# Sharing the first squares of a hybrid attention layer between two engines, moving one weight cast and four differences

## The chip, the cores and the metric

The kernel runs on one core of a Trainium2 chip. The metric is the device time of one execution in microseconds (us). The engines are TensorE (PE; its weight loads are listed apart as PEld), VectorE (DVE), ScalarE (ACT), GpSimd (POOL) and SyncE (SP), which here only issues DMAs. Each engine works through a queue of its own in a fixed order.

## The reference, cut to what matters

One layer, 1,024 positions, width 1,024, all fp32:

```python
h = rms_norm(x, pre_g)                     # x * rsqrt(mean(x*x) + 1e-6) * pre_g
z = jnp.einsum('bsd,de->bse', h, w_in)     # w_in: 1024 x 7184
qa, ka, va, ga, qb, kb, vb, gb, gk_low = split_columns(z)
oa = diff_attention(...)                   # 8 heads, softmax differences
gk = gk_low @ w_gk_up + b_gk               # gk_low has 16 columns
ob = gla_chunked(qb, kb, vb, log_sigmoid(gk) / 16)
y = concat([oa, ob]) @ w_out
return x + rms_norm(y, post_g)
```

The change lies in the first 80 us: the norm of `x`, its transposition, and the beginning of the product with `w_in`.

## The kernel before, in words

**The input.** `x` is loaded in eight tiles of 128 rows by 1,024 columns (`load_x`, L596). For each of the first four, `norm_x` (L613) lets ScalarE square the tile and sum it along the row, then `rstd` (L1633) makes the reciprocal root: two small ScalarE steps (Ln, Exp; L1636, L1637) and three small VectorE steps (L1638, L1640, L1646). `scale_x` (L607) multiplies the tile by it: columns 0 to 511 on VectorE, columns 512 to 1,023 on GpSimd. The other four tiles are normed in pairs, and scaled by GpSimd alone.

**Transposition.** `first(h)` (L654) transposes half h of the columns of tiles 0 to 3 on TensorE into four PSUM banks, and `put` (L644) splits each bank into a high part (`h_hi`, ScalarE, rounded to fp32r, times `pre_g`) and a low part (`h_lo`, VectorE, the rest). `blocks(j)` (L679) does the same for tiles 4 to 7 and also makes sums and differences of the four blocks of `h` (`s1`, `s2`, `s3`, and at L771 `s4`). Products are done by seven block products in place of eight (`LEFT`, L383, says which block each takes), so sums and differences of `w_in` are needed too.

**Weights.** `prepare(i)` (L283) makes the weights of step i of `order` (L243): a ScalarE cast to a high part (L379) and a VectorE subtraction to a low part (L380), after a VectorE subtraction where a difference of blocks is wanted. Steps 0 and 1 share a pair of tiles, as do 2 and 3, so `prepare(0..3)` casts twice. `go(n)` (L739) takes n steps; each prepares up to three steps ahead, then `multiply` (L395) issues 24 or 12 matmuls. TensorE's order is the program's (L142). While `pinned[0]` is set (L638 to `first(1)`, and for the beginning of the first `blocks`), the orders of ScalarE, VectorE and GpSimd are the program's too. Later they are chosen by the compiler's schedule, which goes by its own estimate of times, within the data's dependencies; `issue_after` puts a floor under single instructions.

**Idle products.** `spin` (L388) issues matmuls on a zero tile between the transposes of the first tiles, so that TensorE isn't idle until the first product.

**The low-rank gate.** `low_rank_weights` (L786) loads `w_gk_up` and 16 columns of `w_in` by GpSimd's queue into tiles `gk_up` and `wd`, and splits them on VectorE into `up` (a part of tile `ku`) and `wl`; `low_rank` (L808) multiplies with them.

The order around the change:

```python
for i in range(4):
    prepare(i)
first(0)
norm_x(4, 5)
norm_x(6, 7)
...
go(1)
first(1)
```

Of the kernel before, what the change touches and what calls it, by code (L numbers as in the profile page):

```python
# [8 lines left out]
F32 = mybir.dt.float32  # L9
F32R = mybir.dt.float32r  # L10
AF = mybir.ActivationFunctionType
ALU = mybir.AluOpType
PSUM = bass.MemoryType.PSUM

P = 128
S = 1024
D = 1024
# [5 lines left out]
EPS = 1e-6  # L23
# [8 lines left out]
def hymba_kernel(  # L32
# [20 lines left out]
    nc = tc.nc  # L53
# [21 lines left out]
    act, dve, pool = Queue(nc.scalar), Queue(nc.vector), Queue(nc.gpsimd)  # L75
# [4 lines left out]
    def cols(half):  # L80
        return slice(half * 512, half * 512 + 512)
# [3 lines left out]
    hw = ctx.enter_context(tc.tile_pool(name="hw", bufs=1, side="right", reuse_waits="tile"))  # L85
    const = ctx.enter_context(tc.tile_pool(name="const", bufs=1))
# [8 lines left out]
    eps_t = const.tile([P, 1], F32, name="eps_t")  # L95
# [33 lines left out]
    def bank(i, shape, name):  # L129
        return psum.tile(shape, F32, tag=f"b{i}", name=name)  # L130
# [4 lines left out]
    def take_bank(shape, name):  # L135
        i = free.pop(0)
        return bank(i, shape, name), i
# [3 lines left out]
    def mm(*a, **k):  # L141
        tc.keep_in_program_order(pe.matmul(*a, **k))  # L142

    def tr(dst, src):
        tc.keep_in_program_order(pe.transpose(dst, src, ident))  # L145
# [114 lines left out]
    i = order.index((1, 4))  # L260
# [22 lines left out]
    def prepare(i):  # L283

        if i >= len(order) or i in ws:
            return
        if 4 <= i <= n_early + 1:
            with tc.issue_after(act.last), tc.issue_after(dve.last):
                make_weights(i)
        elif order[i] in ((0, 6), (0, 4)):  # L290
            with tc.issue_after(behind[2 if order[i] == (0, 6) else 0].ins):
                make_weights(i)
        else:
            make_weights(i)
# [44 lines left out]
    def make_weights(i):  # L339
        p, n = order[i]  # L340
        if (wide(p) and p % 2) or p == VALS[1]:
            ws[i] = ws_wide[p - 1, n]
            return
        if p in VALS:
            ws[i] = ws_wide[p, n] = value_weights(n)
            return
        if p in early and n < 3:
            src = early[p][n - 1]
        else:
            fetch_raw(p, n, i)  # L350
            if wide(p):
                (b11, b21), (b12, b22) = ([raws[q].get(kh) for kh in range(2)] for q in (p, p + 1))
            else:
                top, bot = raws[p][0], raws[p][1]
                b11, b12 = top[:, :, :P], top[:, :, P:]
                b21, b22 = bot[:, :, :P], bot[:, :, P:]


            def sub(dst, a, b):
                dve.tensor_tensor(dst, a, b, ALU.subtract)  # L360
                return dst

            if n == 5:
                src = sub(b11, b12, b11)
            elif n == 6:
                src = sub(b11, b22, b11)
            elif n == 4:
                src = sub(b21, b21, b11)
            elif n == 7:
                src = sub(b12, b22, b12)  # L370
            else:
                src = {1: b11, 2: b21, 3: b22}[n]
        if wide(p):
            w = [ap.tile([P, HB, 256], F32R, tag="ring", name="w", bufs=NRING) for _ in range(2)]
            ws_wide[p, n] = w
        else:
            w2 = ap.tile([P, 2, HB, P], F32R, tag="ring", name="w", bufs=NRING)
            w = [w2[:, 0], w2[:, 1]]
        act.copy(w[0], src)  # L379
        dve.tensor_tensor(w[1], src, fp(w[0]), ALU.subtract)  # L380
        ws[i] = w
# [6 lines left out]
    def spin(n):  # L388

        if not spins:  # L390
            spins.append(bank(free[-1], [P, 512], "spin"))
        for i in range(n):
            mm(spins[0], ones, idle, start=(i == 0), stop=(i == n - 1))
# [200 lines left out]
    xs, x2 = [], []  # L594
# [12 lines left out]
    def scale_x(st, cs, engine=pool):  # L607
        x_cs = xs[st][:, cs]
        return engine.tensor_scalar(x_cs, x_cs, norms[st], 1.0, ALU.mult, ALU.mult)

    norms = {}

    def norm_x(*sts):  # L613
        n = len(sts)
        ssq = const.tile([P, 4, n], F32, tag=f"ssq{sts[0]}", name="ssq", bufs=1)
        for i, st in enumerate(sts):
            junk = hw.tile([P, D], F32, tag=("s2_hi0", "s2_lo0")[st % 2], name="junk")
            act.activation(
                junk, xs[st], AF.Square, scale=D**-0.5, accum_out=ssq[:, 0, i : i + 1]
            )  # L620
        rstd(nc, ssq[:, :, :n], ssq[:, 0, :n], eps_t, tc.keep_in_program_order)
        for i, st in enumerate(sts):
            norms[st] = ssq[:, 1, i : i + 1]
            if n == 1:
                scale_x(st, cols(0), dve)
            else:
                scale_x(st, slice(0, D))
# [8 lines left out]
    load_early(2)  # L636
    load_early(4)
    pinned[0] = True  # L638
    for st in range(4):
        norm_x(st)  # L640
    for st in range(4):
        scale_x(st, cols(1))

    def put(ps, k, dst, j):  # L644
        hi, lo = dst
# [6 lines left out]
    f1 = [hpool.tile([P, HB, 512], F32, tag=f"s4_{n}0", name=f"f1{n}") for n in ("hi", "lo")]  # L652

    def first(h):  # L654

        ps = [take_bank([P, 512], "xT") for _ in range(HB)]
        if not h:
            spin(14)
        for i in range(4):
            for j in range(HB):  # L660
                k = h * HB + j
                tr(ps[j][0][:, i * P : (i + 1) * P], xs[i][:, k * P : (k + 1) * P])
            if not h:
                spin((3, 7, 3, 4)[i])
        hi, lo = H[("h11", "h12")[h]]
        for j in range(HB):
            put(ps[j][0], h * HB + j, (hi, lo), j)
        pinned[0] = not h
        for j in range(HB):
            if h:  # L670
                act.activation(f1[h][:, j], ps[j][0], AF.Copy, scale=pre_g[:, h * HB + j : h * HB + j + 1])
            free.append(ps[j][1])
# [78 lines left out]
                if fill and next(fill[0], 0) == 0:  # L751
                    fill.pop(0)

    for i in range(4):
        prepare(i)
    first(0)
    norm_x(4, 5)
    norm_x(6, 7)
    for j in range(HB):
# [11 lines left out]
    s4 = [kp.tile([P, 2, 512], F32, tag=f"k{i}", name="s4") for i in range(2)]  # L771
    with tc.issue_after(behind[0].ins), tc.issue_after(behind[1].ins):
        for j in range(HB):
            dve.tensor_tensor(s4[j // 2][:, j % 2], f1[1][:, j], f1[0][:, j], ALU.subtract)
    for j in range(HB):
        parts("s4", j, s4[j // 2][:, j % 2])

# [3 lines left out]
    up, keep = ku[:, 0], fp(ku)[:, 1]  # L781

    wl2 = kp.tile([P, KT + HB, 64], F32R, tag="q0", name="wl2")
    R = GK_RANK

    def low_rank_weights():  # L786

        pool.memset(keep, 1.0)
        pool.memset(keep.rearrange("p (c i) -> p c i", i=64)[:, :, 0:1], 0.0)
        gk_up = t_c("gk_up")[:R]  # L790
        pool.dma_start(gk_up, w_gk_up[0])
        wd = t_c("wd").rearrange("p (k r) -> p k r", r=R)
        wd, wl = wd[:, KT : KT + HB], wd[:, :KT]
        pool.dma_start(wl, w_in[0, :, GKL : GKL + GK_RANK].rearrange("(k p) c -> p k c", p=P))
        pool.memset(fp(wl2), 0.0)
        pool.memset(fp(gkl), 0.0)
        pool.memset(fp(up), 0.0)
        with tc.issue_after(behind[0].ins):
            dve.tensor_tensor(wd, wl[:, HB:], wl[:, :HB], ALU.subtract)
            for dst, src in ((wl2[:, :KT], wl), (wl2[:, KT:], wd)):  # L800
                dve.tensor_copy(dst[:, :, :R], src)
                dve.tensor_tensor(dst[:, :, 32 : 32 + R], src, fp(dst[:, :, :R]), ALU.subtract)
            dve.tensor_copy(up[0:R], gk_up)
            dve.tensor_copy(up[32 : 32 + R], gk_up)
            dve.tensor_tensor(up[64 : 64 + R], gk_up, fp(up[0:R]), ALU.subtract)
            dve.tensor_tensor(up[96 : 96 + R], gk_up, fp(up[0:R]), ALU.subtract)

# [825 lines left out]
def rstd(nc, t, s, eps, pin=None):  # L1633

    pin = pin or (lambda ins: ins)
    pin(nc.scalar.activation(t[:, 1], s, AF.Ln, bias=eps))  # L1636
    exp = pin(nc.scalar.activation(t[:, 1], t[:, 1], AF.Exp, scale=-0.5))  # L1637
    half = pin(nc.vector.tensor_scalar(t[:, 2], s, eps, -0.5, ALU.add, ALU.mult))  # L1638
    if t.shape[2] == 1:
        pin(nc.vector.scalar_tensor_tensor(  # L1640
            t[:, 2], t[:, 1], t[:, 2], t[:, 1], ALU.mult, ALU.mult
        ))
    else:
        pin(nc.vector.tensor_tensor(t[:, 2], t[:, 2], t[:, 1], ALU.mult))
        pin(nc.vector.tensor_tensor(t[:, 2], t[:, 2], t[:, 1], ALU.mult))
    last = nc.vector.scalar_tensor_tensor(  # L1646
        t[:, 1], t[:, 2], 1.5, t[:, 1], ALU.add, ALU.mult
    )
    return exp, pin(last), half
# [32 lines left out]
```

## Time and profile before

| | us |
|---|---|
| median of three runs | 973.23 (973.07 to 973.25) |
| span of the profiled execution, first to last instruction | 971.1 |
| TensorE busy / VectorE / ScalarE / GpSimd | 958.7 / 735.5 / 604.6 / 207.9 |
| first product on real data | begins at 13.70 |
| low-rank product | begins at 74.13 |

For the profiled execution itself no time beside its span is listed; the median of the runs lies 2.1 us above the span. Times in the profile count from the span's first instruction. A group's line has the busy time, the mean of one instruction in ns, and the idle time of the engine before them with what ended it. In a timeline, a row has start, length, engine, line, operation, output and inputs, and in brackets the idle time ahead of it. Nearly all ScalarE, VectorE and GpSimd work is recorded under L66, since it passes through one helper; tiles tell it apart. The shapes read "partitions x columns". A sum along the row shows as a second small instruction behind the main one (`ACTIVATION_READ_ACCUMULATOR` on ScalarE, `DVE_READ_ACCUMULATOR2_ANT` on VectorE); the kernel's existing `tensor_tensor_reduce` shows as `CUSTOM_DVE_ANT_0`.

### The profile page before, as it was taken

The page shows a single profiled execution, that of the slowest core. Times are in us where ns is not written, and L with a number is a line of the kernel's source. Part 1 is how long each engine was busy: PE and PEld are TensorE (multiplying, and loading weights), DVE is VectorE, ACT ScalarE, POOL GpSimd, SP SyncE. Part 2 cuts the span into 40 slices and gives each one's busy share as a digit, 9 for nine tenths or more (in the row PEclk, how much of TensorE's full clock was granted, in tenths as well). Part 3 has the DMA queues.
Part 4 walks back from the last instruction along what each step waited for, and adds up shares of the span by engine and source line. Part 5 has one row for each costly group of instructions (what it writes and reads, how often), then busy time and mean ns, then how long its engine had stood idle before and what let it go on. Part 6 is the DMA issues. An engine that isn't in the chain of part 4 may idle for free.

```text
span 971.1 us, 15096 instructions
## 1 busy us (share of the span) xinstructions
PE 958.7 (99%) x4977; PEld 814.5 (84%) x4977; DVE 735.5 (76%) x1464; ACT 604.6 (62%) x1166; POOL 207.9 (21%) x266
## 2 busy tenths in 40 slices
PE   8999999999999999999999999999999999999997
PEld 7998988888888888888888888878888888888786
DVE  5996698897687686686766576587888888898554
ACT  8752364764667555576665344366786787887773
POOL 4300001212141221231100002121322222443322
PEclk9999999999999999999999999999999999999999
DMA  9433366578568987986754588996656769994777
GB/s 347 163 103 117 101 192 225 170 239 294 199 210 255 300 272 251 302 277 212 259 177 152 163 251 269 401 336 203 221 170 218 241 200 355 334 286 106 152 210 148
DMA packets 151293, 220.39 MB, mean 227 GB/s; under 512 B 15728, under 2 KB 86384, under 8 KB 151120
## 3 DMA queue, kind: packets, MB, share of 16 engines
q1 hardware_dynamic: 137056, 178.70, 56.8%
q0 software_dynamic: 14160, 40.74, 14.5%
q8 instruction: 39, 0.64, 0.3%
q14 instruction: 38, 0.31, 0.1%
HBM read 133.93 MB, written 88.60 MB: 229 GB/s over the span
## 4 chain that ended last, share of the span: by engine, by line
PE 94%; ACT 3%; DVE 1%; issue 1%; DMA 0%; POOL 0%; DVEq 0%; ACTq 0%; POOLq 0%
PE x L142 23%; PE z L142 16%; PE y L142 16%; PE ypart L142 13%; PE sc L142 7%; PE po L142 5%; PE yps L142 4%; PE wtr L145 3%; PE gpo L142 3%; PE kv L142 1%; ACT junk L66 1%; PE gkl_ps L142 1%; PE pa L142 1%; DVE p L66 1%; ACT h_hi L66 0%
## 5 line engine op out<-in xcount | busy, mean ns | idle before, releaser
L66 ACT CAST w<-w_raw 128x512 fp32r<-128x512 f32 (+1 forms) x150 | 98.0, 655 | 92.3 <-PE y L142 46.4
L66 DVE TENSOR_TENSOR w<-w_raw,w 128x512 fp32r<-128x512 f32 (+1 forms) x150 | 109.3, 732 | 48.8 <-ACT w L66 44.6
L66 ACT ACTIVATE p<-p,stt 128x896 f32<-128x896 f32 (+7 forms) x128 | 99.3, 777 | 36.2 <-DVE stt L66 35.2
L66 ACT COPY s<-x 128x512 f32<-128x512 f32 x82 | 47.8, 586 | 88.8 <-PE x L142 88.2
L66 POOL TENSOR_SCALAR p<-p,stt,lam 128x1024 f32<-128x1024 f32 (+3 forms) x64 | 56.2, 879 | 147.7 <-DVE stt L66 143.8
L66 DVE CUSTOM_DVE_ANT_0 p<-sc,maskt 128x512 f32<-128x512 f32 (+3 forms) x128 | 74.3, 585 | 14.2 <-PE sc L142 12.9
L66 POOL DMA_DIRECT2D wo_d<-wo_hi x32 | 17.5, 545 | 313.9 <-ACT wo_hi L66 313.9
L142 PE MATMUL z<-s_hi,w 128*128 128x512 f32 x320 | 80.2, 393 | 0.0
L142 PE MATMUL x<-s_hi,w 128*128 128x512 f32 x320 | 80.1, 392 | 0.0
L142 PE MATMUL y<-h_hi,w 128*128 128x512 f32 x320 | 80.0, 392 | 0.0
L142 PE MATMUL ypart<-wo_hi,m_hi 128*128 128x512 f32 x192 | 79.5, 414 | 0.1
L142 PE MATMUL ypart<-wo_hi,m_lo 128*128 128x512 f32 x192 | 75.5, 393 | 0.0
L142 PE MATMUL ypart<-wo_lo,m_hi 128*128 128x512 f32 x192 | 75.4, 393 | 0.0
L142 PE MATMUL sc<-k,q 128*128 128x512 f32 (+1 forms) x192 | 69.1, 363 | 1.4 <-DVE stt L66 1.3
L142 PEld LDWEIGHTS z<-s_hi,w 128*128 128x128 f32 x320 | 59.7, 188 | 12.3
L142 PEld LDWEIGHTS y<-h_hi,w 128*128 128x128 f32 x320 | 59.7, 188 | 12.3
L142 PEld LDWEIGHTS x<-s_hi,w 128*128 128x128 f32 x320 | 59.7, 188 | 12.3
L66 DVE TENSOR_TENSOR w_raw<-w_raw 128x512 f32<-128x512 f32 (+1 forms) x88 | 66.1, 751 | 1.9 <-DMA w_raw<-in_w_in_dram 0.8
L142 PE MATMUL sc<-ks,q 128*128 128x512 f32 (+1 forms) x192 | 66.0, 347 | 0.0
L66 ACT CAST wt_hi<-wtr 128x512 fp32r<-128x512 f32 (+1 forms) x80 | 42.8, 535 | 25.1 <-PE wtr L145 24.3
L66 DVE TENSOR_TENSOR wt_lo<-wtr,wt_hi 128x512 fp32r<-128x512 f32 (+1 forms) x80 | 50.6, 633 | 8.9 <-ACT wt_hi L66 8.2
L66 DVE TENSOR_TENSOR c<-z,s 128x512 f32<-128x512 f32 x48 | 32.8, 688 | 30.6 <-ACT s L66 20.3
(225 smaller groups left out, 2351.7 us busy)
## 6 DMA issues: line engine op xcount, KB each, us to landing
w_raw<-in_w_in_dram SPq DMA_DIRECT2D x48, 512.0 KB, 4.9
wo_d<-wo_hi POOLq DMA_DIRECT2D x32, 256.0 KB, 3.8
q<-q_d SPq DMA_DIRECT2D x32, 256.0 KB, 4.7
k<-k_d SPq DMA_DIRECT2D x32, 256.0 KB, 5.5
ks<-k_d SPq DMA_DIRECT2D x64, 128.0 KB, 6.0
v<-v_d SPq DMA_DIRECT2D x16, 512.0 KB, 7.0
wo_raw<-in_w_out_dram POOLq DMA_DIRECT2D x31, 256.0 KB, 4.8
wo_d<-gqd POOLq DMA_DIRECT2D x22, 256.0 KB, 4.2
```

Of the source, the lines that this page charges most:

```text
L66: ins = op(*a, **k)
L142: tc.keep_in_program_order(pe.matmul(*a, **k))
L145: tc.keep_in_program_order(pe.transpose(dst, src, ident))
```

## The change

Five edits. (1) The loop over the first four tiles becomes `norm_first`: ScalarE squares the whole of tile 0 and the left halves of tiles 2 and 3; VectorE squares and sums, by `tensor_tensor_reduce`, the whole of tile 1 and the right halves of tiles 2 and 3. A right half's sum starts from 1e-6 and stands in for the epsilon of `rstd`. Tiles 0 and 1 have their left columns scaled by GpSimd, tiles 2 and 3 by VectorE. (2) The idle products are 18, 1, 1, 1, 3 instead of 14, 3, 7, 3, 4. (3) `prepare(2)` and `prepare(3)` stand behind `first(0)`. (4) The four differences `s4` are made by GpSimd. (5) Two copies of `gk_up` into `up` are made by ScalarE.

```diff
-    for st in range(4):
-        norm_x(st)
-    for st in range(4):
-        scale_x(st, cols(1))
+    def square(st, half, s, init):
+        cs = cols(half)
+        junk = hw.tile([P, 512], F32, tag=("s1_lo0", "s1_lo1")[half], name="junk_h")
+        if half:
+            dve.tensor_tensor_reduce(
+                junk, xs[st][:, cs], xs[st][:, cs], 1.0 / D, init, ALU.mult, ALU.add, s
+            )
+        else:
+            act.activation(junk, xs[st][:, cs], AF.Square, scale=D**-0.5, accum_out=s)
+
+    def norm_first():
+
+        ssq = [const.tile([P, 5, 1], F32, tag=f"ssq{st}", name="ssq", bufs=1) for st in range(4)]
+        whole = hw.tile([P, D], F32, tag="s2_hi0", name="junk")
+        act.activation(whole, xs[0], AF.Square, scale=D**-0.5, accum_out=ssq[0][:, 0])
+        whole = hw.tile([P, D], F32, tag="s2_lo0", name="junk")
+        dve.tensor_tensor_reduce(
+            whole, xs[1], xs[1], 1.0 / D, 0.0, ALU.mult, ALU.add, ssq[1][:, 0]
+        )
+        for st in range(4):
+            t = ssq[st]
+            eps = eps_t if st < 2 else t[:, 4]
+            if st == 1:
+                square(2, 1, ssq[2][:, 4], EPS)
+            elif st > 1:
+                square(st, 0, t[:, 0], None)
+            if st == 2:
+                square(3, 1, ssq[3][:, 4], EPS)
+            rstd(nc, t[:, :4], t[:, 0], eps, tc.keep_in_program_order)
+            norms[st] = t[:, 1]
+            scale_x(st, cols(0), dve if st > 1 else pool)
+        for st in range(4):
+            scale_x(st, cols(1))
+
+    norm_first()
...
-            spin(14)
+            spin(18)
...
-                spin((3, 7, 3, 4)[i])
+                spin((1, 1, 1, 3)[i])
...
-    for i in range(4):
+    for i in range(2):
         prepare(i)
     first(0)
+    for i in range(2, 4):
+        prepare(i)
...
-            dve.tensor_tensor(s4[j // 2][:, j % 2], f1[1][:, j], f1[0][:, j], ALU.subtract)
+            pool.tensor_tensor(s4[j // 2][:, j % 2], f1[1][:, j], f1[0][:, j], ALU.subtract)
...
-            dve.tensor_copy(up[0:R], gk_up)
-            dve.tensor_copy(up[32 : 32 + R], gk_up)
+            act.copy(up[0:R], gk_up)
+            act.copy(up[32 : 32 + R], gk_up)
```

## The prediction

> **What bounds the kernel now.** I read the page first, for the busy shares and the chain that ended last.
>
> ```profile
> span 971.1 us, 15096 instructions
> PE 958.7 (99%) x4977; PEld 814.5 (84%) x4977; DVE 735.5 (76%) x1464; ACT 604.6 (62%) x1166; POOL 207.9 (21%) x266
> PE 94%; ACT 3%; DVE 1%; issue 1%; DMA 0%; POOL 0%; DVEq 0%; ACTq 0%; POOLq 0%
> ```
>
> TensorE carries 94% of the chain and is busy 99% of the span, so only time in which TensorE stands still can be won, and 971.1 - 958.7 = 12.4 us of it exist. The change touches the first 75 us alone; the second view, busy time by stretches, shows where the standstills are (columns: stretch, length, then busy time and instructions of PE, PEld, DVE, ACT, POOL, granted clock, DMA share, GB/s).
>
> ```profile
> 13.60:24.00 10.40, 10.11 (x75) 8.99 (x75) 8.19 (x18) 10.27 (x22) 4.41 (x4) 1.00 1.11 405
> 24.00:58.00 34.00, 33.92 (x261) 32.35 (x260) 32.59 (x45) 23.38 (x39) 10.93 (x12) 1.00 0.43 136
> 58.00:63.60 5.60, 4.56 (x40) 4.36 (x38) 5.54 (x11) 4.44 (x7) 0.00 (x0) 1.00 0.52 140
> 63.60:971.10 907.50, 898.79 (x4562) 760.27 (x4562) 683.41 (x1377) 556.50 (x1081) 186.62 (x235) 1.00 0.72 228
> ```
>
> Up to 13.6 us there is no product yet. From 13.6 to 24 us ScalarE is full (10.27 of 10.40). From 24 to 58 us TensorE is full and VectorE nearly so. From 58 to 63.6 us TensorE loses 1.04 us while VectorE is full. So a change of this part acts through two places. The chain, in order of time, and the weight loads show both.
>
> ```profile
> 13.05 2.32 ACT h_hi L66 x4
> 15.38 2.08 ACT junk L66 x4
> ...
> 21.13 2.33 ACT h_hi L66 x4
> ```
>
> ```profile
> 23.51 0.65 PEld L142 LDWEIGHTS y<-w,h_hi 128*128 128x128 f32 x5 [0.28 <-ACT h_hi L66]
> ...
> 61.32 1.03 PEld L142 LDWEIGHTS y<-w,h_hi 128*128 128x128 f32 x8
> 63.60 0.53 PEld L142 LDWEIGHTS y<-w,h_hi 128*128 128x128 f32 x4 [1.24 <-DVE w L66]
> ```
>
> First place: until 23.5 us ScalarE's queue sets the pace, its last piece being the second group of block casts (`h_hi` from 21.13), which TensorE already awaits by 0.28 us. Second place: at 63.60 TensorE waits 1.24 us for a low weight part from VectorE.
>
> **Part 1, squares shared, second weight cast moved.** The rows of the last tile of the four, and what follows:
>
> ```profile
> 9.47 1.04 ACT L66 ACTIVATE junk<-x 128x1024 f32<-128x1024 f32 x1
> 10.64 0.21 DVE L1638 TENSOR_SCALAR ssq<-ssq,eps_t 128x1 f32<-128x1 f32 x1
> 11.08 1.98 ACT L66 CAST w<-w_raw 128x1024 fp32r<-128x1024 f32 x2
> 11.20 0.22 DVE L1640 SCALAR_TENSOR_TENSOR ssq<-ssq 128x1 f32<-128x1 f32 x1 [0.35 <-ACT ssq L1637]
> 11.46 0.16 DVE L1646 SCALAR_TENSOR_TENSOR ssq<-ssq 128x1 f32<-128x1 f32 x1
> 11.65 0.49 DVE L66 TENSOR_SCALAR x<-x,ssq 128x512 f32<-128x512 f32 x1
> 11.77 0.93 POOL L66 TENSOR_SCALAR x<-x,ssq 128x512 f32<-128x512 f32 x1 [0.68 <-ACT ssq L1637]
> 12.14 1.63 DVE L66 TENSOR_TENSOR w<-w_raw,w 128x1024 fp32r<-128x1024 f32 x1
> 12.19 0.42 PEld L145 LDWEIGHTS xT<-ident,x 128*128 128x128 f32 x4 [0.23 <-DVE x L66]
> 12.96 2.41 ACT L66 ACTIVATE h_hi<-xT,pre_g 128x512 fp32r<-128x512 f32 x4
> ```
>
> ScalarE now does four whole squares one after the other; each ends in two small activations and three small VectorE steps. In the new order VectorE takes the whole of tile 1 and a half each of tiles 2 and 3, all in one fixed queue with the small steps of every tile. The nearest rows for the new reduction are the kernel's own, on one operand in PSUM and one in SBUF, and a two-operand step of 1,024 columns:
>
> ```profile
> L66 DVE CUSTOM_DVE_ANT_0 p<-sc,maskt 128x512 f32<-128x512 f32 x80 | 54.9, 686 | 12.6 <-PE sc L142 11.9
> L66 DVE DVE_READ_ACCUMULATOR2_ANT stt<- 128x1 f32 x192 | 15.9, 83 | 0.0
> L66 DVE TENSOR_TENSOR t<-b,t 128x1024 f32<-128x1024 f32 x4 | 4.9, 1220 | 0.2 <-ACT t L66 0.2
> ```
>
> A half is 0.69 + 0.08 = 0.77 us, a whole 1.22 + 0.08 = 1.30 us. It can't begin before tile 1 is there (row of its load alone: issued at 1.3, 4.6 us to landing, so 5.9):
>
> ```profile
> L604 SPq DMA_DIRECT2D x<-in_x_dram x1: 415/415/415, 1.3 to 1.3; - x1
> ...
> DMA to landing us min/median/max: 4.6/4.6/4.6
> ```
>
> The small steps of one tile take 0.24 (the 0.21 step and a gap), 11.46 - 11.20 = 0.26 and 11.65 - 11.46 = 0.19: 0.69 us. VectorE then runs: tile 1 whole to 7.2; steps of tile 0 to 7.9; half of tile 2 to 8.65; steps of tile 1 to 9.35; half of tile 3 to 10.1; steps of tile 2 to 10.8; its scaling (0.49) to 11.3; steps of tile 3 to 12.0; its scaling to 12.5. Today that last scaling ends at 11.65 + 0.49 = 12.14. So sharing gains nothing: ScalarE is relieved and VectorE becomes the longer queue. One cost comes on top. Tiles 0 and 1 are now scaled by GpSimd, 0.93 us each, right while VectorE reduces two SBUF operands; the step at 12.14 took 1.63 instead of some 1.22 us with 0.56 us of such a GpSimd scaling beside it. Ends: nothing, or 0.4 for each of two reductions. I take 0.4, as that row is the same pair of operations: tile 3 is scaled at 13.3.
>
> From there to the first block cast is 0.45 us (four transposes, 0.42 at 12.19, and a step to ScalarE): 13.75, against 12.96 today; without contention 12.95. Today the second weight cast (half of 1.98, 1.0 us) lies ahead of the block casts and covers the transposes. In the new order ScalarE idles there and does that cast behind the block casts, ahead of the four squares at 15.38, which it delays, and with them all that leads to `h_hi` at 21.13. Behind the first block cast ScalarE's queue is full today, so the shift at 23.5 us is 13.75 - 12.96 + 1.0 = **+1.8 us** (without contention +1.0). The moved step issues no load of its own (its half of `w_raw` was fetched before), and its low part on VectorE, now behind the low parts of the blocks, is wanted only by the step at 23.5. Low parts of the blocks that come earlier on VectorE are worth nothing, as TensorE waits at 23.5 anyway. From 24 us on all three engines move together, and no slack is left in which it could be absorbed.
>
> The warm-up products (24 in place of 31, thinly spread) cost nothing of themselves, since TensorE idles between tiles. Should the granted clock (1.00 in all rows above) fall for it, the first two steps would run slower under the cover of ScalarE, whose queue would be over 1.8 us behind TensorE's; beyond that it would show.
>
> **Part 2, differences to GpSimd, two copies to ScalarE.** The rows around the second standstill, and those from which GpSimd is priced:
>
> ```profile
> 24.01 6.47 POOL L66 TENSOR_TENSOR f1hi<-h_hi,h_lo 128x512 f32<-128x512 f32 x4
> 24.42 1.96 DVE L66 TENSOR_TENSOR w<-w_early,w 128x1024 fp32r<-128x1024 f32 x1
> ...
> 55.27 1.21 DVE L66 TENSOR_TENSOR w<-w_raw,w 128x1024 fp32r<-128x1024 f32 x1
> 55.37 0.98 POOL L66 DMA_DIRECT2D wd<-in_w_in_dram  x1 [3.72 <-DVE s_lo L66]
> 57.01 0.68 DVE L66 TENSOR_TENSOR s_lo<-f1hi,s_hi 128x512 fp32r<-128x512 f32 x1
> 58.75 2.49 DVE L66 TENSOR_TENSOR s<-f1lo,f1hi 128x512 f32<-128x512 f32 x4
> 58.76 0.59 ACT L66 COPY s<-x 128x512 f32<-128x512 f32 x1 [3.36 <-PE x L142]
> 59.24 2.00 ACT L66 CAST w<-w_raw 128x1024 fp32r<-128x1024 f32 x2
> 61.16 0.86 DVE L66 CAST ku<-gk_up 16x512 fp32r<-16x512 f32 x2
> 62.32 2.35 DVE L66 TENSOR_TENSOR w<-w_raw,w 128x1024 fp32r<-128x1024 f32 x2
> 65.85 1.05 ACT L66 CAST w<-w_raw 128x1024 fp32r<-128x1024 f32 x1 [1.55 <-DVE w_raw L66]
> ```
>
> VectorE loses 2.49 us of differences and 0.86 us of copies just ahead of the awaited low part (first of the two at 62.32). That part then needs only its high part, the first ScalarE cast, ready at 59.24 + 1.00 = 60.24. Beside GpSimd's differences (four for 6.47, 1.62 each) it takes 1.96 as at 24.42, alone 1.21: done at 61.5 to 62.2. TensorE wants it when the eight loads at 61.32 are through, 62.35. So the 1.24 us go in full: **-1.24 us**; the least, if VectorE puts another slowed step first, is nothing. ScalarE's two copies, by the 0.59 of a copy at 58.76 some 1.2 us, fit in its idle time there (3.36 and 1.55 us). The casts of the four differences now wait for GpSimd until about 66 us; behind them in ScalarE's queue is the weight cast at 65.85, which has 1.55 us of idle time ahead of it. What is late next is TensorE itself, full after 63.6.
>
> **Sum.** 1.79 - 1.24 = +0.55 us, between -0.2 and +1.8. No time is listed for the profiled execution by itself; its span is 971.1, the median of the three runs 973.23, and I leave the 2.1 us around the span as they are. 973.23 + 0.55 = **973.8**. About 0.2% (1.95 us) is what a measurement of this kernel can tell from no change, so the forecast is no change.
>
> **Rivals.**
>
> *Head start.* If VectorE's queue is shorter than I add it up, ScalarE bounds: its last square, begun at 9.47, is a half and some 0.5 us shorter, so the weight cast that today begins at 11.08 begins at 10.6 and ends at 11.6, and blocks begin there instead of at 12.96. With the moved cast that is -1.35 + 1.0 = -0.35, with the stall -1.6: 971.6, at best, with the squares ahead shorter too, 971.0. Against it: the rows of the small steps add up to four times 0.69 whatever the reductions take.
>
> *The stall stays.* If a step slowed by GpSimd stands ahead of the low part, the margin of 0.15 us (62.35 - 62.2) is gone, and +1.8 stands alone: 975.0.
>
> [...]
>
> *A load behind the differences* (slower). The load of `wd` is issued by GpSimd at 55.37; the differences can start at 57.01 + 0.68 = 57.7. Were they queued ahead, the load would go out 6.5 us later, at 64.2, and the small casts that VectorE has just ahead of 62.32 would hold up the low part by some 5 us: 979. The order of the rows speaks against it.
>
> **Chances.** Forecast 0.55 (its own range 972.9 to 974.5), head start 0.15, stall stays 0.11, half rate 0.13, load behind 0.06. Faster by over 0.2% needs under 971.3: a third of the head start, and some reordering of the unpinned queues: 0.08. Slower needs over 975.2: most of the half rate, the load behind, a quarter of the stall: 0.19. Within: 0.73. The range runs from 971.4 to 976.1; outside are the load behind (0.06), the lower end of the head start (0.05) and the upper half of the half rate (0.06).
>
> **What would show it.** Right: two-part rows of the new reduction near 1.3 and 0.77 to 1.2 us; tile 3's scaling at 12.5 to 13.3; the first block cast at 12.95 to 13.75, with ScalarE idle ahead of it; one weight cast behind the block casts; `y` at 23.51 moved to 24.5 to 25.3; no wait for `w` near 63 to 65. Wrong: tile 3 scaled before 11.5; a reduction of 1,024 columns at 2.4 us; a wait on `wd`; or a difference that first appears after 80 us, which would mean that the order of the other queues changed.

## The result, and the profile after

The changed kernel takes 978.58 us (median of five runs, 978.05 to 980.01) against 973.23 before: a ratio of 1.0059, interval 1.0047 to 1.0072. It is slower, by 5.35 us of the medians, and lies outside the predicted range. The profiled execution took 978.05 us, its span is 976.0, so what lies around the span is 2.05 us, as before; the loss is inside the span, 4.9 us. Beside the medians of before in the experiments below (972.71 to 972.90) the ratio is the number to compare.

The page of the changed kernel, span, busy time and chain by engine:

```profile
span 976.0 us, 15086 instructions
PE 959.8 (98%) x4970; PEld 815.2 (84%) x4970; DVE 738.2 (76%) x1462; ACT 603.8 (62%) x1166; POOL 219.9 (23%) x272
...
PE 92%; DVE 3%; ACT 2%; issue 1%; DMA 1%; POOL 1%; SPq 0%; DVEq 0%; ACTq 0%; POOLq 0%
```

TensorE is busy 1.1 us longer for seven instructions less, and stands still 976.0 - 959.8 = 16.2 us instead of 12.4. The longer busy time goes with a lower granted clock: 1.00 in all the stretches of before, it reads 0.84, 0.98 and 0.60 in stretches shown below. GpSimd has 12 us more to do, while four differences at the row of before (1.62 each) would be 6.5; its four difference rows, shown below, add up to 13.1. Two of the stretches of busy time that were shown of before:

```profile
24.00:58.00 34.00, 32.55 (x242) 30.48 (x242) 32.15 (x43) 24.00 (x40) 22.87 (x15) 1.00 0.38 126
58.00:63.60 5.60, 3.02 (x20) 2.81 (x19) 5.49 (x7) 3.03 (x6) 2.72 (x3) 0.84 0.22 51
```

From 24 to 58 us TensorE, full before (33.92 of 34.00), now misses 1.45 us, and GpSimd is busy 22.87 us instead of 10.93, although the differences were expected behind 57.7. From 58 to 63.6 us TensorE works 3.02 us instead of 4.56, and the granted clock is 0.84 instead of 1.00. A finer cut of the same view:

```profile
55.00:62.00 7.00, 4.51 (x38) 4.30 (x36) 6.89 (x8) 3.63 (x6) 5.72 (x4) 0.98 0.02 7
62.00:66.00 4.00, 3.91 (x21) 3.91 (x22) 3.92 (x6) 2.32 (x6) 0.00 (x0) 0.60 0.77 170
```

TensorE stands still for 2.5 us before 62, and then works for 4 us at a mean granted clock of 0.60. The low clock itself is 0.50, from 61.76 to 65.17; the slice takes in 0.83 us at 1.00 behind it. The weight loads name what it waited for:

```profile
25.30 1.25 PEld L142 LDWEIGHTS y<-w,h_hi 128*128 128x128 f32 x10 [0.28 <-ACT h_hi L66]
...
53.49 1.26 PEld L142 LDWEIGHTS z<-w,s_hi 128*128 128x128 f32 x10 [1.34 <-ACT s_hi L66]
...
62.09 2.21 PEld L142 LDWEIGHTS x<-w,s_hi 128*128 128x128 f32 x10 [2.79 <-ACT s_hi L66]
...
69.70 1.01 PEld L142 LDWEIGHTS y<-w,h_hi 128*128 128x128 f32 x8 [0.20 <-DVE w L66]
```

Two waits are new, both for `s_hi`, the high part of a sum of blocks that ScalarE casts. The ten loads at 62.09 took 2.21 us; ten loads at 53.49 took 1.26. Weight loads of the two traces, paired one to one in TensorE's order, give the whole loss:

| place | before | after | later by | added there |
|---|---|---|---|---|
| `y`, behind the second block casts | 23.51 | 25.30 | 1.79 | +1.79 |
| `z`, first wait for `s_hi` | 50.30 | 53.49 | 3.19 | +1.40 |
| `x`, second wait for `s_hi` | 56.06 | 62.09 | 6.03 | +2.84 |
| `x`, under the low clock | 58.08 | 65.23 | 7.15 | +1.12 |
| `y`, where `w` was awaited | 63.60 | 69.70 | 6.10 | -1.05 |
| end of the span | 971.12 | 976.02 | 4.90 | -1.20 |

The last line is the sum of small waits in the score products from 640 us on, which fall differently in every kernel. The first line is what was forecast, the fifth is the gain that was forecast; the three between are the miss, 5.36 us. GpSimd's own rows are where they begin:

```profile
40.37 6.03 POOL L66 TENSOR_TENSOR s<-f1lo,f1hi 128x512 f32<-128x512 f32 x1
...
47.25 1.45 POOL L66 TENSOR_TENSOR s<-f1lo,f1hi 128x512 f32<-128x512 f32 x1
53.47 4.02 POOL L66 TENSOR_TENSOR s<-f1lo,f1hi 128x512 f32<-128x512 f32 x1 [4.77 <-DVE f1hi L66]
57.43 0.72 POOL L66 DMA_DIRECT2D gk_up<-in_w_gk_up_dram  x1
58.73 1.64 POOL L66 TENSOR_TENSOR s<-f1lo,f1hi 128x512 f32<-128x512 f32 x1 [0.58 <-DVE f1hi L66]
60.33 0.98 POOL L66 DMA_DIRECT2D wd<-in_w_in_dram  x1
```

The floor under the differences is gone: `behind` names steps of VectorE, and on GpSimd it held nothing, so the first difference runs at 40.37, ahead of both loads. It takes 6.03 us, the third 4.02, the second 1.45 for the same operation. The third also waits 4.77 us for a block of `f1hi` that VectorE writes only then. Both loads, independent of all this, stand behind. In the trace of before the first of them went out here:

```profile
50.92 0.73 POOL L66 DMA_DIRECT2D gk_up<-in_w_gk_up_dram  x1 [9.45 <-DVE s_lo L66]
```

It is 6.5 us late. The chain of the changed kernel, in order of time, carries that to TensorE:

```profile
53.47 3.96 POOL s L66
57.43 2.12 DMA gk_up<-in_w_gk_up_dram
...
59.63 0.09 ACT ku L66
...
60.26 0.62 ACT ku L66
...
60.90 0.63 ACT qk_hi L66
61.53 0.52 ACT s_hi L66
...
62.09 6.65 PE x L142 x42
```

A stretched difference, the load behind it, the two copies of `gk_up` that the change gave to ScalarE, and behind them in ScalarE's queue the cast that TensorE awaits. The first wait, at 53.49, has another road; VectorE and ScalarE in the same trace:

```profile
45.77 1.17 DVE L66 TENSOR_TENSOR h_lo<-h,h_hi 128x512 fp32r<-128x512 f32 x1
...
47.47 1.78 DVE L66 TENSOR_TENSOR h<-f1hi,h 128x512 f32<-128x512 f32 x1
...
59.16 2.29 DVE L66 TENSOR_TENSOR w<-w_raw,w 128x1024 fp32r<-128x1024 f32 x1
59.63 1.25 ACT L66 CAST ku<-gk_up 16x512 fp32r<-16x512 f32 x2 [2.22 <-DMA gk_up<-in_w_gk_up_dram]
```

The like VectorE steps of 512 columns take 0.68 or 0.69 us in the other rows from 38 to 66 us (one more, at 56.85 beside the third difference, took 1.19); the first two, beside GpSimd's first and second difference, take 1.17 and 1.78, and the 1,024-column step at 59.16 takes 2.29 instead of 1.21. The first two make everything behind them in VectorE's queue 0.49 + 1.10 = 1.6 us later, the sum whose cast TensorE awaits at 53.49 among it.

The theory from these rows: the head cost what was added up, and the differences on GpSimd cost the rest, in two ways, by the loads queued behind them and by slowing VectorE. Rivals: that ScalarE's copies are to blame, that the load alone is, or that the head costs more than its 1.8 us.

### The profile page after: what moved, and what is told of

Same layout as the page of the kernel before. It is cut to its first block, busy times and chain, and to the rows that moved or that the text cites. A ratio compares the mean times of both kernels' runs of the same rounds, so it can differ in the third digit from the quotient of the medians.

```text
span 976.0 us, 15086 instructions
## 1 busy us (share of the span) xinstructions
PE 959.8 (98%) x4970; PEld 815.2 (84%) x4970; DVE 738.2 (76%) x1462; ACT 603.8 (62%) x1166; POOL 219.9 (23%) x272
## 4 chain that ended last, share of the span: by engine, by line
PE 92%; DVE 3%; ACT 2%; issue 1%; DMA 1%; POOL 1%; SPq 0%; DVEq 0%; ACTq 0%; POOLq 0%
PE x L142 22%; PE z L142 15%; PE y L142 14%; PE ypart L142 13%; PE sc L142 7%; PE po L142 5%; PE yps L142 4%; PE wtr L145 3%; PE gpo L142 3%; PE kv L142 1%; PE gkl_ps L142 1%; PE pa L142 1%; DMA x<-in_x_dram 1%; ACT h_hi L66 0%; ACT junk L66 0%
```

## The experiments

"Later by" below means the paired weight loads against before, as in the table. From 640 us on, the waits in the score products differ from kernel to kernel: by the paired loads at 300 and 960 us, that part gave the profiled executions between a gain of 1.23 us on before (`e6_squares`) and a loss of 1.19 (`e2_copies_back`). So a microsecond in the medians says little of the first 75 us by itself; the paired loads do.

**Take back one of the two late edits, or both.** `e1_head` puts differences and copies back on VectorE, `e2_copies_back` the copies alone, `e3_diff_back` the differences alone:

```diff
-            pool.tensor_tensor(s4[j // 2][:, j % 2], f1[1][:, j], f1[0][:, j], ALU.subtract)
+            dve.tensor_tensor(s4[j // 2][:, j % 2], f1[1][:, j], f1[0][:, j], ALU.subtract)
...
-            act.copy(up[0:R], gk_up)
+            dve.tensor_copy(up[0:R], gk_up)
```

Expected of the first: 

> The changed kernel with the four differences and the two copies back on VectorE: only the shared squares, the idle products and the moved cast are left. Theory (the loss comes from GpSimd's queue: the differences stand ahead of the load of gk_up, and ScalarE's copy of it holds up the casts behind it): the step y still comes 1.8 us later than before, the waits of TensorE for s_hi (1.3 and 2.8 us) and the dip of the clock behind them are gone, the old wait of 1.2 us for w is back; 974 to 975. Rival (the later head itself upsets the queues behind it): still over 977.

Measured: 974.78, ratio 1.0019 (1.0010 to 1.0029). TensorE is 1.63 us later at `y` and stays so; the wait for `w` is back (1.25 us at 65.22); no wait for `s_hi` remains. The expectation holds.

Expected of the second: 

> The changed kernel with only the two copies of gk_up back on VectorE; the differences stay on GpSimd. Theory: the 2.8 us wait at x goes from ScalarE, and the clock stays at 1.00; the 1.3 us wait at z stays, since the differences still slow VectorE; 974.5 to 975.5, if VectorE isn't held up by the same late load in ScalarE's place. [...]

Measured: 982.16, ratio 1.0101 (1.0084 to 1.0118), a miss. Without the copies ScalarE casts `s_hi` at 58.44, in time, but TensorE waits all the same:

```profile
58.93 2.29 DVE L66 TENSOR_TENSOR w<-w_raw,w 128x1024 fp32r<-128x1024 f32 x1
61.27 1.01 PEld L142 LDWEIGHTS x<-w,s_hi 128*128 128x128 f32 x8 [1.86 <-DVE w L66]
```

Behind the late `s_hi` stood a late `w`: the step on VectorE that ran into the fourth difference. With the copies back on VectorE, `w` is late once more, at 70.15 (wait 1.58). Of the 2.8 us by which its profiled span exceeds that of the change, only 0.45 are there before 640 us; the rest are waits in the scores.

Expected of the third: 

> The changed kernel with only the four differences back on VectorE; the copies stay on ScalarE. Theory: gk_up is loaded near 52 us again, both waits for s_hi are gone and the clock stays at 1.00; the old wait for w is at most the 1.2 us of before; 973.5 to 975. Rival (the copies on ScalarE cost in themselves, by their place in its queue): a wait for s_hi of a microsecond or more stays, over 975.5.

Measured: 974.96, ratio 1.0024 (1.0013 to 1.0035). Both long waits for `s_hi` are gone and `gk_up` is loaded at 52.54. So the differences on GpSimd cost 0.0035 of the time, 3.4 us. The copies on ScalarE cost nothing that the medians can tell (1.0024 against 1.0019), but the wait for `w`, expected at 1.2 us at most, became longer:

```profile
63.11 1.38 DVE L66 TENSOR_TENSOR ku<-gk_up,ku 16x512 fp32r<-16x512 f32 x2
...
66.07 1.01 PEld L142 LDWEIGHTS y<-w,h_hi 128*128 128x128 f32 x8 [1.85 <-DVE w L66]
```

TensorE is 2.47 us later than before there, against 1.63 in `e1_head`. Of these 0.85 us, 0.25 arise at the step `x`: ScalarE makes the copies at 54.74, ahead of a weight cast that then runs at 56.02 instead of 54.61. The other 0.6 come from VectorE: two subtractions that need the copies, at 67.47 and behind the awaited low part in `e1_head`, now stand ahead of it and take 1.38 us where the copies took 0.86.

**Is it the loads behind the differences?** `e4_behind_loads` gives GpSimd the differences after its two loads; `e10_sp_load` leaves them where they are and lets SyncE issue the load of `gk_up`.

```diff
-        pool.dma_start(wl, w_in[0, :, GKL : GKL + GK_RANK].rearrange("(k p) c -> p k c", p=P))
+        gk_load[:] = [pool.dma_start(wl, w_in[0, :, GKL : GKL + GK_RANK].rearrange("(k p) c -> p k c", p=P)).ins]
...
     low_rank_weights()
+    s4 = [kp.tile([P, 2, 512], F32, tag=f"k{i}", name="s4") for i in range(2)]
+    with tc.issue_after(gk_load[0]):
+        for j in range(HB):
+            pool.tensor_tensor(s4[j // 2][:, j % 2], f1[1][:, j], f1[0][:, j], ALU.subtract)
```

Expected: 

> The changed kernel, but the four differences are put behind GpSimd's two loads in its queue, so that they start near 58 us or later as the prediction had assumed. Theory: no wait for s_hi, none for w, the head's 1.8 us alone less the old wait of 1.2 us: 973 to 974.2. Rival (what counts is that GpSimd's two-operand steps slow VectorE, wherever they stand): a wait of a microsecond or more near 58 to 66 us, 975 or more.

Measured: 980.98, ratio 1.0084 (1.0069 to 1.0099), a miss. The loads are early again and the wait at `z` is gone (TensorE is 1.76 us later there, as at `y`), but the kernel is no faster than the change. Its timeline:

```profile
57.15 0.97 POOL L66 DMA_DIRECT2D wd<-in_w_in_dram  x1 [3.73 <-DVE s_lo L66]
57.27 6.89 DVE L66 TENSOR_TENSOR w<-w_raw,w 128x1024 fp32r<-128x1024 f32 x1
...
58.13 4.93 POOL L66 TENSOR_TENSOR s<-f1lo,f1hi 128x512 f32<-128x512 f32 x4
...
64.21 1.78 PEld L142 LDWEIGHTS x<-w,s_hi 128*128 128x128 f32 x8 [5.59 <-DVE w L66]
```

One VectorE step of 1.2 us takes 6.89, until GpSimd is through with all four differences, which run at 1.23 us each. TensorE waits 5.59 us for it. The rows don't show a sharing of a rate, in which both would be slowed: the step took 5.7 us longer than its like, the differences were the shortest of all those timed here on GpSimd (1.23 against 1.44 to 6.03 us). One of the two was shut out while the other ran, here over four instructions in a row. In the changed kernel VectorE, dense with steps, was the one that held and GpSimd's first difference the one shut out (6.03 us).

`e10_sp_load` is one line:

```diff
-        pool.dma_start(gk_up, w_gk_up[0])
+        sp.dma_start(gk_up, w_gk_up[0])
```

Expected: 

> The changed kernel with the load of gk_up moved from GpSimd's queue to SyncE's; the differences stay on GpSimd, the copies on ScalarE. Theory (of the two causes of the wait at x, the late gk_up sets its length): gk_up is there by 56 us, the cast of s_hi that ended the wait moves from 61.4 to 58.5, and what is left at x is a wait of some 1.8 us for w, since VectorE's low part is shut out by the fourth difference; 977 to 978. Rival (shutting out alone sets it): 2.8 us again, within 0.5 us of 978.6.

Measured: 979.75, ratio 1.0073 (1.0060 to 1.0085), a miss. The copies run at 56.23, `s_hi` at 59.00, and TensorE waits 1.87 us for `w` in place of 2.79 for `s_hi`. The wait became smaller where expected, the time did not: the head of this run was 0.3 us later, the low clock, a mean of 0.61 from 62.70 to 67.10, cost 1.5 us (later by 5.29 at 61.82, 6.77 at 68.09), and `w` was awaited once more, for 0.69 us. So the load alone isn't the cause either.

**Is it that both read the same memory?** `e7_memset` is `e4_behind_loads` with four memsets of 128 x 1,024 in place of the four differences: GpSimd is busy at the same place, but writes only. This kernel leaves out the values of one block.

```diff
-            pool.tensor_tensor(s4[j // 2][:, j % 2], f1[1][:, j], f1[0][:, j], ALU.subtract)
+            pool.memset(s4[j // 2], 0.0)
```

Expected: 

> As e4_behind_loads, but the four differences on GpSimd are replaced by four memsets of 128 by 1,024, which read nothing and take about as long in sum (3.8 us); the values of one block are left out. Theory now, after e4 (GpSimd and VectorE shut each other out while both read SBUF, GpSimd with its operands and VectorE with two): VectorE's step at 57 us takes 1.2 us again in place of 6.9, the wait of 5.6 us at x is gone and the clock stays at 1.00; 973 to 975. Rival (VectorE or TensorE waited there for something else, the order of the queues above all): the wait stays over 3 us; 978 or more.

Measured: 975.92, ratio 1.0032 (1.0019 to 1.0045). GpSimd's row and VectorE's:

```profile
57.61 3.65 POOL L66 MEMSET s<- 128x1024 f32 x4
```

```profile
56.82 1.22 DVE L66 TENSOR_TENSOR w<-w_raw,w 128x1024 fp32r<-128x1024 f32 x1 [0.21 <-ACT w L66]
...
59.17 1.21 DVE L66 TENSOR_TENSOR w_raw<-w_raw 128x1024 f32<-128x1024 f32 x1
```

Beside 3.65 us of memsets VectorE's steps take 1.22 and 1.21 us (the first step meets them at its end, the second in its whole length), the 5.59 us wait is gone, and no low clock shows: sixteen weight loads at 60.02 take 1.99 us, as at 58.44 before, and from 64 to 76 us the clock reads 1.00. By this comparison, 6.89 us beside differences and 1.22 beside memsets, it was GpSimd's reading that shut VectorE out, not its being busy or its writing. 975.9 is above what was expected, with a wait of 1.68 us for `w` at 68.50 that was not followed up.

Nor was the step that was listed first the one that ran through: in `e4_behind_loads` VectorE's is listed from 57.27, before the first difference at 58.13, and still ended behind the fourth.

**The two halves of the head.** `e5_cast` is the kernel before with the second weight cast moved alone, `e6_squares` with the shared squares and the idle products alone, both casts ahead of the blocks.

```diff
-    for i in range(4):
+    for i in range(2):
         prepare(i)
     first(0)
+    for i in range(2, 4):
+        prepare(i)
```

Expected: 

> The kernel before with the moved weight cast alone. Theory (ScalarE's queue sets the pace to 23.5 us): blocks begin 0.4 us earlier, at 12.55, since tile 3 is scaled at 12.14 as before; the cast, 1.0 us, then stands ahead of the next four squares, and the last weight load that waits for h_hi moves from 23.51 to 24.1; 973.3 to 974. Rival (the cast is hidden behind the blocks and the earlier start counts): that load at 23.5 or earlier, 973.2 or less.

Measured: 973.61, ratio 1.0008 (0.9999 to 1.0017); later at `y` by 0.58. Blocks begin at 12.59, 0.37 earlier, the cast stands at 14.88.

Expected: 

> The kernel before with the shared squares and the new idle products alone; both weight casts stay ahead of the blocks. Theory: tile 3 is scaled at 13.3 to 13.4, the second cast is covered by that, blocks begin at 13.8, and the last wait for h_hi moves from 23.51 to 24.3; 973.5 to 974.5. Rival (the whole 1.8 us of the head comes from one of the two edits): 25.1 or more here, or 23.6 or less.

Measured: 973.64, ratio 1.0007 (0.9998 to 1.0016); later at `y` by 0.76, blocks at 13.72. VectorE in this kernel:

```profile
9.16 0.68 DVE L66 CUSTOM_DVE_ANT_0 junk_h<-x 128x512 f32<-128x512 f32 x1
...
10.44 0.63 DVE L1677 SCALAR_TENSOR_TENSOR ssq<-ssq 128x1 f32<-128x1 f32 x1
11.11 0.91 DVE L66 TENSOR_SCALAR x<-x,ssq 128x512 f32<-128x512 f32 x1
...
12.81 0.49 DVE L66 TENSOR_SCALAR x<-x,ssq 128x512 f32<-128x512 f32 x1
```

A step on one column takes 0.63 us, its like 0.16; a scaling 0.91, its like 0.49. Both stand beside GpSimd's scalings. `e9_scale_order` tests that by reversing the order in which GpSimd scales the right halves, so that it waits for the last tile first and begins when VectorE has done its small steps:

```diff
-        for st in range(4):
+        for st in (3, 2, 1, 0):
             scale_x(st, cols(1))
```

Expected: 

> As e6_squares, but GpSimd scales the right halves of the first tiles in the order 3, 2, 1, 0, so that it can't start on them before VectorE's last small step. Theory (GpSimd's scalings run into VectorE's small steps and its scaling of tile 2, which took 0.91 in place of 0.49 us): tile 3 is scaled at 12.4 to 12.7 instead of 13.3, blocks begin at 13.2, held by the second weight cast, and the last wait for h_hi is at 23.7 instead of 24.3; 972.8 to 973.4. Rival (the steps are that long of themselves): 24.2 to 24.3 again.

Measured: 972.20, ratio 0.9995 (0.9986 to 1.0004), below what was expected. The same rows:

```profile
10.28 0.16 DVE L1677 SCALAR_TENSOR_TENSOR ssq<-ssq 128x1 f32<-128x1 f32 x1
10.48 0.48 DVE L66 TENSOR_SCALAR x<-x,ssq 128x512 f32<-128x512 f32 x1
...
11.64 0.49 DVE L66 TENSOR_SCALAR x<-x,ssq 128x512 f32<-128x512 f32 x1
```

Tile 3 is scaled 1.17 us earlier than in `e6_squares`, and TensorE is 0.40 us earlier than before at `y` instead of 0.76 later.

**The differences later, on VectorE.** `e11_head_late` is the change with this alone; `e8_late` is the kernel before with this and the copies on ScalarE; `e12_best` adds the head of `e9_scale_order` to `e8_late`.

```diff
-    with tc.issue_after(behind[0].ins), tc.issue_after(behind[1].ins):
...
     low_rank_weights()
     go(4)
+    s4 = [kp.tile([P, 2, 512], F32, tag=f"k{i}", name="s4") for i in range(2)]
+    with tc.issue_after(dve.latest):
+        for j in range(HB):
+            dve.tensor_tensor(s4[j // 2][:, j % 2], f1[1][:, j], f1[0][:, j], ALU.subtract)
```

Expected: 

> The changed kernel with the differences on VectorE, put 15 us later in its queue as in e8_late; head and copies as changed. Theory (the prediction's sum was right but for GpSimd): TensorE is 1.6 to 1.8 us late at 24.7 us and 0.6 to 0.8 us late behind 70 us; 972.5 to 973.5. Rival (the later head takes the gain of e8_late away, because VectorE is late with something else): over 1.3 us late behind 70 us; 974 or more.

Measured: 973.87, ratio 1.0006 (0.9997 to 1.0015). TensorE is 1.48 us late at `y` and 0.52 behind the place where `w` was awaited: the forecast's sum was +0.55. With GpSimd out of it, the forecast for both places nearly holds. The time is above the 972.5 to 973.5 expected, and not to be told from before.

Expected: 

> The kernel before with the four differences left on VectorE but put some 15 us later in its queue (they are first used near 88 us), and the two copies of gk_up on ScalarE; nothing else. Theory (the old wait of 1.2 us comes from these steps standing ahead of the awaited low part): no wait for w near 63.6, TensorE 1.2 us earlier from there; 972 to 972.8, less if later waits give it back. Rival (VectorE is simply full up to there and something else is late next): 973 or more.

Measured: 971.52, ratio 0.9984 (0.9975 to 0.9993), faster than before by 1.35 us. VectorE's rows:

```profile
60.80 1.22 DVE L66 TENSOR_TENSOR w<-w_raw,w 128x1024 fp32r<-128x1024 f32 x1
...
76.02 2.48 DVE L66 TENSOR_TENSOR s<-f1lo,f1hi 128x512 f32<-128x512 f32 x4
```

The differences still take 2.48 us of VectorE, at 76.02, where nobody waits; the awaited low part is done at 60.80 + 1.22 = 62.02, ahead of the load that takes it at 62.55, and TensorE is 1.05 us earlier behind that place. The profiled execution gained another 0.9 in the scores.

Expected: 

> The kernel before with the shared squares, GpSimd scaling the right halves in the order 3, 2, 1, 0, both weight casts ahead of the blocks, the differences late on VectorE and the two copies on ScalarE. If the two places act one by one: -0.4 us at 23.5 from the head, -1.05 more behind 63.6 from the wait for w that goes, so about -1.5 on TensorE at 70 us, and 970.5 to 971.6 by what the scores add. Rival: a gain in the head is given back at the next full engine, so that TensorE stands at about -1.05 behind 70 us as with the late differences alone, and the time is 971.5 or more.

Measured: 970.90, ratio 0.9983 (0.9974 to 0.9992), faster than before, not to be told from `e8_late`. TensorE is 0.33 us early at `y`, 0.22 late at 56.28 (a wait of 0.27 for `s_hi`, behind ScalarE's copies as in `e8_late`, which is 0.51 late there), and 1.34 early where `w` was awaited. So in the traces the two gains add: 1.05 in `e8_late` and 0.35 in `e9_scale_order` at that place. The medians can't tell 0.3 us.

## Why the prediction was wrong, point by point

**Part 1, the head: right in its path, with its size made up differently.** +1.8 us at 23.5 was forecast, +1.79 measured. VectorE and ScalarE in the changed kernel:

```profile
5.87 1.23 DVE L66 CUSTOM_DVE_ANT_0 junk<-x 128x1024 f32<-128x1024 f32 x1 [5.87 <-DMA x<-in_x_dram]
...
10.53 0.63 DVE L1679 SCALAR_TENSOR_TENSOR ssq<-ssq 128x1 f32<-128x1 f32 x1
...
11.20 0.91 DVE L66 TENSOR_SCALAR x<-x,ssq 128x512 f32<-128x512 f32 x1
...
12.89 0.49 DVE L66 TENSOR_SCALAR x<-x,ssq 128x512 f32<-128x512 f32 x1
...
13.80 2.42 ACT L66 ACTIVATE h_hi<-xT,pre_g 128x512 fp32r<-128x512 f32 x4 [1.88 <-PE xT L145]
```

Tile 3 is scaled at 12.89 + 0.49 = 13.38 (forecast 13.3), the first block cast starts at 13.80 (13.75) with ScalarE idle ahead of it. But the 0.8 us of contention is not on the two reductions, which run at 1.23 and 0.69 us, as the rows of before had them; it is on a small step (0.63 for 0.16) and a scaling (0.91 for 0.49), 0.89 us. `e9_scale_order` shows it as GpSimd's scalings. That GpSimd's scalings meet VectorE was right, the rows that they meet were not; that 0.89 came so near to the 0.8 taken is luck.

**The reduction at half rate: refuted.** It was given 0.13, and the 2.3 us from the forecast of 973.8 to the range's upper end of 976.1 stand for it; no run shows them. The reduction of 1,024 columns, with both operands in SBUF in fp32, took 1.23 us, where 2.4 was named as the sign of it. **Head start: refuted**, as VectorE's queue was as long as added up.

**Part 2, the differences: the step that failed.** The prediction let them begin at 57.7, because VectorE had them there, and let them slow a VectorE step from 1.21 to 1.96 us. Both were wrong. The place: the first ran at 40.37, since the floor that held them on VectorE did not hold GpSimd; two loads came to stand behind them. The price: GpSimd's difference and VectorE's step didn't slow each other a little, they shut each other out: a difference of 1.23 us took 6.03 (changed kernel), a VectorE step of 1.21 took 6.89 (`e4_behind_loads`). The row at 24.42, on which 1.96 rested, showed one outcome of such a meeting and not its bound. The 1.62 us for GpSimd was not the least either: in `e4_behind_loads`, with VectorE shut out, a difference took 1.23.

**The load behind the differences**, given 0.06 and 979 us, came nearest, for the mechanism too: the loads did go out behind differences. Two things in it were otherwise: the load of `gk_up` mattered, not that of `wd`, and it reached TensorE by ScalarE's copies, not by VectorE's casts. "The order of the rows speaks against it" was the false sentence: the order on one engine's queue says nothing of what another engine's queue will look like once the instructions are moved there. Its own sum slipped as well: 64.2 is 8.8 us behind 55.37, not 6.5, which is the length of four differences; measured, the load of `gk_up` went out 6.5 us late and that of `wd` 5.0. So 979 lies by the measured 978.6 in part by luck. And the load isn't enough: with the load out of the way (`e10_sp_load`, `e4_behind_loads`) the shutting out alone left the kernel as slow (979.75 and 980.98 us against 978.58).

**The copies at no cost: not so in the traces.** They were to fit into ScalarE's idle time behind 55.4; they ran at 54.74, ahead of a weight cast, and let two other steps of VectorE in ahead of the awaited low part. TensorE is 0.85 us later for it (`e3_diff_back` against `e1_head`); the medians can't tell it. In the changed kernel they also carried the late `gk_up` to TensorE. **The gain of 1.24: right in mechanism.** The wait for `w` shrinks to 0.20; in `e8_late` and `e11_head_late`, where the differences leave that place without going to GpSimd, TensorE gains 1.55 us and more from 56.06 to 63.60, some 0.5 of it making up for a loss that these kernels have just ahead of 56.06, behind ScalarE's copies. No run has the differences later with the copies left on VectorE.

**The sum.** +1.79 - 1.05 is +0.74; the forecast was +0.55. What was missing is 5.36 us of waits and low clock, of which `e3_diff_back`, with the differences on VectorE again, has 0.25 left at the same place; and 1.20 us less of waits in the scores, on which the forecast said nothing.

## What to carry to other kernels

An instruction that is moved to another engine leaves its floors and its neighbours behind: look up its place in the new queue and what stands behind it there, DMA issues first, and what moves up in the queue that it left. Before work goes to an idle GpSimd, list the VectorE steps that run meanwhile: in `e4_behind_loads` one of them, with two operands in SBUF, took 6.89 us instead of 1.2, until GpSimd was through with its four differences. Cheaper than another engine was another time: the same 2.5 us on VectorE, 15 us later, gave the gain that the move was meant to give.

## What the runs showed of the hardware

Shutting out did not end with the instruction that held: VectorE's step stayed out over four differences in a row (6.89 us instead of 1.22, `e4_behind_loads`), and a difference stayed out over a dense row of VectorE steps (6.03 us instead of 1.23, changed kernel). What two of the differences waited for can be read from VectorE's rows of the changed kernel:

```profile
45.17 0.68 DVE L66 TENSOR_TENSOR gv_st<-y,s 128x512 f32<-128x512 f32 x1
...
56.25 0.68 DVE L66 TENSOR_TENSOR c<-y,s 128x512 f32<-128x512 f32 x1
```

The first and third difference end at 46.40 and 57.49. Less the 1.23 us that one took with VectorE shut out, their work begins at 45.17 and 56.26, just where VectorE comes to a step that reads `y`, a product in PSUM, in place of a second operand in SBUF. The second row and the third difference meet alike in `e2_copies_back` (56.02 + 1.23 = 57.25; the difference ends at 57.26) and in `e10_sp_load` (56.56 + 1.23 = 57.79, and 57.79). This is a reading of four meetings; no run moved an operand to test it. The second and the fourth difference (1.45 and 1.64 us) got in sooner, between two steps with both operands in SBUF; why, no run here shows.

The granted clock fell in or behind a standstill, but not by its length alone. In `e2_copies_back` it fell behind a wait of 1.86 us at 61.27, in `e3_diff_back` a wait of 1.85 us at 66.07 left it whole:

```profile
61.20:62.20 1.00, 0.92 (x7) 0.93 (x8) 1.00 (x3) 0.00 (x0) 0.00 (x0) 1.00 0.37 66
62.20:66.50 4.30, 4.30 (x26) 4.30 (x25) 4.22 (x9) 3.60 (x6) 0.00 (x0) 0.60 0.65 170
```

```profile
66.00:68.00 2.00, 1.93 (x16) 1.93 (x17) 2.00 (x3) 0.17 (x1) 0.00 (x0) 1.00 0.30 66
```

In the changed kernel it was 0.50 for 3.4 us, from 61.76 to 65.17. With 0.50 for the low clock, the means of the stretches give the same 3.4 us for `e2_copies_back` (0.60 over 4.3 us) and for `e10_sp_load` (0.61 over 4.4 us), and 6.8 for `e4_behind_loads` (0.69 over 6.2 us and 0.54 over the next 3.2); these three are estimates. In `e2_copies_back` the clock still read 1.00 up to 62.20, 0.9 us after the products had resumed. Waits of 1.86 to 2.79 us were enough here, and 5.59 in `e4_behind_loads`; what set the wait of 1.85 us in `e3_diff_back` apart from these, no run here shows.
